# Two of the four weight-side sums of a Strassen product move from VectorE to adding DMAs

## The chip, the cores and the metric

The kernel runs on one core of one Trainium2 chip. The metric is the device time of one execution in microseconds (us): the median of the runs, three of the kernel before. Engines: TensorE (PE; its weight loads are PEld), VectorE (DVE), ScalarE (ACT), GpSimd (POOL) and SyncE (SP), which here issues all DMAs of the kernel before.

## What is computed

One decoder block: RMSNorm of 528 tokens (16 meta tokens and 512), one wide projection `w_in`, two gated branches (differential attention, and a state-space branch with a short convolution and chunked scan, called SSD), one projection each, a gated merge, an output projection and a last RMSNorm. Cut to the matrix products, which are the bulk:

```python
u = rmsnorm(h, norm_g[l])
zp = u @ w_in[l]                       # 2048 x 13344
q, k, v, g_att, z_ssm, xbc, dt, m_att, m_ssm = jnp.split(zp, SPLIT_IDX, axis=-1)
...
y_att = oa @ w_br_attn[l]              # 1024 x 2048
...
y_ssm = yg @ w_br_ssm[l]               # 2048 x 2048
merged = jax.nn.sigmoid(m_att) * y_att + jax.nn.sigmoid(m_ssm) * y_ssm
h = h + merged @ w_out[l]              # 2048 x 2048
return rmsnorm(h[:, N_META:], final_g)
```

## The kernel before, in words

**Jobs.** `plan()` (line 61) lists jobs; each makes 256 output features for all tokens. A job of form "S" is one Strassen-Winograd product (`strassen`, line 211): its weights are cut into A11 A12 / A21 A22, the activations into B11 B12 / B21 B22, and seven products P1 to P7 take the place of eight. The activation sums T1 to T4 are made once per matrix; the weight sums are made per job. Jobs of form "F" (`plain`, line 340) multiply without Strassen: one gate job, all y_att jobs, the first output job. Stages follow each other: attention heads (jobs kv and qg), gates, the convolution (jobs bc and xs), gates and z with the SSD chunks as side work, y_att, y_ssm, output.

**Weights.** Every tile is 128 x 1024 float32, 512 KB, one quadrant A of an S job. `pump` (line 154) loads them in the order of `plan()` from SP into five buffers `w` and never runs more than five ahead of `release` (line 162). A sixth buffer, `S`, holds a running weight sum.

**A unit.** Half a tile (512 columns, four weight blocks of 128) is a unit; a job has 14, two per product, in the order P1 P5 P6 P7 P4 P2 P3 (line 49). A unit has three steps, given out by `dense` (line 416): `sums` (line 225), then at most two units later `prep`, then at most three units later `mm`. `prep` calls `split` (line 166): ACT rounds the weights to a high part `wh` (line 170), DVE subtracts for the low part `wl` (line 171). `mm` (line 322) gives TensorE 12 matmuls, three per weight block (high by high, high by low, low by high), 256 or 264 columns wide. `post` (line 272) takes a product from PSUM and adds it on. `later(fn, n)` (line 384) runs something n units on.

**The weight sums before**, all on DVE, for a usual S job (line 225): at P5, S = A21 + A22 (group S<-w, line 184); at P6, S = S - A11; at P7, A21 = A11 - A21 (group w<-w, line 181); at P3, A12 = A12 - S. Two half-tile instructions each. Two jobs go another way: the first (kv 0, `start`, because activations are not ready) and the last (out 7, `end`); 64 are usual.

**Queues.** DVE, ACT, POOL and SP each work in their own order; a waiting instruction holds those behind it. The order in each queue is set by the build's scheduler, from the order in which the code gives the steps out.

**SSD side work** (line 1032). Per chunk SP loads among others `mm` (line 1023, 512 KB, a row of decay sums given to all 128 partitions) and `ea` (line 1027); ACT turns `mm` into decays (line 1067); `wh` of the next units stands behind it in ACT's order.

Of the kernel before, what the change touches and what calls it, by code (L numbers as in the profile page):

```python
# [10 lines left out]
F32 = mybir.dt.float32  # L11
# [25 lines left out]
C_B, C_C, C_DT, C_MA, C_MS = 8192, 8704, 9216, 9248, 11296  # L37

# [75 lines left out]
def block_kernel(ctx, tc, t_in, out):  # L114
# [35 lines left out]
    WB = 5  # L150
    wt = {}
    wstate = {"next": 0, "done": 0}

    def pump(most=1 << 30):
        while wstate["next"] < min(wstate["done"] + WB, n_tiles, most):
            i = wstate["next"]
            w = wp.tile([P, 1024], F32, tag="w", bufs=WB, name="w")
            sp.dma_start(w, wd[i])
            wt[i] = w
            wstate["next"] += 1  # L160

# [49 lines left out]
    def strassen(ji, width, lo, dst, fin, add=None, end=None, start=False):  # L211
# [7 lines left out]
        order = ORDER_START if start else ORDER_END if end else ORDER  # L219

# [4 lines left out]
        def sums(p, u):  # L225

            us = slice(u * 512, (u + 1) * 512)
            pump()
            if start and p == "P3":
                if u == 0:  # L230
                    st["S"] = wp.tile([P, 1024], F32, tag="S", bufs=1, name="S")
                vsub(block("A21", u), block("A11", u), block("A21", u))
                vsub(st["S"][:, us], block("A22", u), block("A21", u))
                vsub(block("A12", u), block("A12", u), st["S"][:, us])
            elif start:
                if p == "P5":
# [7 lines left out]
            if start:
                pass
            elif p == "P6":
                vsub(st["S"][:, us], st["S"][:, us], block("A11", u))
            elif p == "P7":
                vsub(block("A21", u), block("A11", u), block("A21", u))
            elif p == "P3":  # L250
                vsub(block("A12", u), block("A12", u), st["S"][:, us])

        def prep(p, u):
            pump()
            if p in ("P5", "P6"):
                return split(st["S"][:, u * 512:(u + 1) * 512])
            r = split(block({"P1": "A11", "P7": "A21", "P4": "A22", "P2": "A12", "P3": "A12"}[p], u))
            if u == nu - 1 and not end:
                release(({"P7": 2, "P4": 2} if start else {"P7": 2, "P4": 1, "P3": 1}).get(p, 0))
            return r  # L260
# [11 lines left out]
        def post(p, ps):  # L272
            a = ps[:, :width]
            if p == "P1":
                act.activation(ctile("c1"), a, AF.Copy)
            elif start and p != "P4":
                if p == "P2":
                    vadd(ctile("u3"), a, st["c1"][:, :width])
                elif p == "P3":
                    act.activation(ctile("c5"), a, AF.Copy)  # L280
                elif p == "P6":
                    vadd(ctile("u2"), a, st["c1"][:, :width])
                    d = dst(0, 0)
                    act.activation(d, st["u3"][:, :width], AF.Copy)
                    fin(0, 0, d)
                elif p == "P5":
                    act.activation(ctile("c1"), a, AF.Copy)
                    vadd(ctile("u4"), a, st["u2"][:, :width])
                    quadrant(0, 1, add, st["u4"], st["c5"])
                else:  # L290
                    vadd(ctile("u3"), a, st["u2"][:, :width])
                    quadrant(1, 1, add, st["u3"], st["c1"])
            elif end and p in ("P6", "P7", "P3", "P5"):
                if p == "P6":
                    vadd(ctile("u2"), a, st["c1"][:, :width])
                elif p == "P7":
                    vadd(ctile("u3"), a, st["u2"][:, :width])
                elif p == "P3":
                    vadd(ctile("u4"), a, st["u2"][:, :width])
                    end(0, 1, st["u4"][:, :width])  # L300
                    end(1, 1, st["u3"][:, :width])
                else:
                    for f, b in ((1, "u3"), (0, "u4")):
                        vadd(dst(f, 1), a, st[b][:, :width])
                    for f in (1, 0):
                        fin(f, 1, dst(f, 1))
            elif p == "P5":
                act.activation(ctile("c5"), a, AF.Copy)
            elif p == "P6":
                vadd(ctile("u2"), a, st["c1"][:, :width])  # L310
                add(ctile("u4"), st["u2"][:, :width], st["c5"][:, :width])
            elif p == "P7":
                vadd(ctile("u3"), a, st["u2"][:, :width])
# [5 lines left out]
            else:  # L319
                quadrant(0, 1, vadd, a, st["u4"])  # L320
# [171 lines left out]
    quad_load(("B21", "B22"), HK[1])  # L492

# [130 lines left out]
    def dt_mm(w):  # L624
# [8 lines left out]
        release()  # L633
# [765 lines left out]
```

## Time and profile before

| | |
|---|---|
| median of 3 runs | 1822.39 us (1817.94 to 1826.14) |
| the profiled execution | 1822.93 us, its span 1821.2 us |
| TensorE busy | 1704.3 us, 94% |
| DVE busy | 1647.5 us, 90% |
| ACT busy | 984.7 us, 54% |
| POOL busy | 569.6 us, 31% |
| DMA engines | 41.3% of 16 engines' time, 240.76 MB on SP's queue |
| mean granted clock of TensorE | 0.978 |

Stages in the span, roughly: start 0 to 100 us, attention 100 to 550, gates to 590, convolution to 865, SSD with z and gates to 1370, y_att to 1460, y_ssm to 1630, output to the end. Shares of busy time are means over these stages, so the tables by stretch matter more. Matmuls are pipelined and their ends are modelled: a busy TensorE still tells that work was there, and the count of matmuls per stretch tells how fast it went.

### The profile page before, as it was taken

How to read it: one execution, taken by the hardware profiler on the slowest of the kernel's cores; microseconds unless marked ns; L12 is line 12 of the kernel's file. 1: busy time of each engine (PE TensorE's matmuls, PEld its weight loads, DVE VectorE, ACT ScalarE, POOL GpSimd, SP SyncE). 2: the span in 40 equal slices, each digit the busy share in tenths (PEclk: the TensorE clock that was granted, in tenths of full speed). 3: DMA queues.
4: the chain of work that ended last, by engine and by line, in shares of the span. 5: the costliest groups of instructions: out<-in, count | busy, mean ns of one | idle time of the engine just before them, and what ended most of it. 6: DMA issues, size and time to landing. Idle time of an engine off the chain costs nothing.

```text
span 1821.2 us, 36122 instructions
## 1 busy us (share of the span) xinstructions
PE 1704.3 (94%) x13523; PEld 1628.8 (89%) x13523; DVE 1647.5 (90%) x2914; ACT 984.7 (54%) x2038; POOL 569.6 (31%) x537
## 2 busy tenths in 40 slices
PE   7799999999999999999998999899998999989996
PEld 6799988899999888888987898899997999979995
DVE  8899888889898999999978898999987499998997
ACT  5655554555555544444575556656563254455653
POOL 3333122212212544442133423513432012134444
PEclk9899999999999999999999999999999999989998
DMA  8222222222233333334455555644466644533443
GB/s 308 86 96 83 81 77 86 78 93 75 76 123 99 108 117 116 118 117 137 155 166 153 159 154 161 188 136 137 159 220 226 190 146 153 174 103 105 134 139 104
DMA packets 136767, 243.06 MB, mean 133 GB/s; under 512 B 15088, under 2 KB 78768, under 8 KB 136080
## 3 DMA queue, kind: packets, MB, share of 16 engines
q1 hardware_dynamic: 136592, 240.76, 41.3%
q8 instruction: 106, 1.74, 0.4%
q14 instruction: 69, 0.57, 0.1%
HBM read 206.83 MB, written 33.88 MB: 132 GB/s over the span
## 4 chain that ended last, share of the span: by engine, by line
PE 33%; DVE 8%; DMA 4%; ACT 3%; issue 2%; POOL 1%; SPq 0%; DVEq 0%; ACTq 0%
PE d_ps L331 26%; PE d_ps L370 4%; DVE wl L171 3%; DMA mm<-d_acs 2%; ACT mm L1067 1%; ACT wh L170 1%; PE s_ps L1104 1%; DVE w L181 1%; DMA ea<-d_acs 1%; DVE res L1337 0%; PE s_ps L1080 0%; POOL mq L178 0%; DVE y L455 0%; DVE S L181 0%; DVE x L455 0%
## 5 line engine op out<-in xcount | busy, mean ns | idle before, releaser
L331 PE MATMUL d_ps<-x,wh 128*128 128x256 f32 (+1 forms) x4224 | 780.2, 286 | 12.7 <-ACT wh L170 10.8
L331 PEld LDWEIGHTS d_ps<-x,wh 128*128 128x128 f32 x4224 | 657.3, 191 | 21.2 <-ACT wh L170 15.1
L331 PE MATMUL d_ps<-x,wl 128*128 128x256 f32 (+1 forms) x2112 | 603.1, 288 | 19.0 <-DVE wl L171 18.7
L331 PE MATMUL d_ps<-y,wh 128*128 128x256 f32 (+1 forms) x3168 | 591.3, 286 | 26.3 <-ACT wh L170 26.3
L170 ACT ACTIVATE wh<-w 128x512 fp32r<-128x512 f32 x708 | 427.0, 625 | 344.4 <-PE d_ps L331 165.2
L171 DVE TENSOR_TENSOR wl<-w,wh 128x512 fp32r<-128x512 f32 x708 | 523.3, 757 | 63.2 <-ACT wh L170 61.7
L331 PEld LDWEIGHTS d_ps<-y,wh 128*128 128x128 f32 x3168 | 490.2, 189 | 41.3 <-ACT wh L170 35.0
L331 PE MATMUL d_ps<-y,wl 128*128 128x256 f32 (+1 forms) x1584 | 447.3, 286 | 2.6 <-DVE wl L171 2.5
L331 PEld LDWEIGHTS d_ps<-x,wl 128*128 128x128 f32 x2112 | 400.9, 191 | 27.5 <-DVE wl L171 25.2
L331 PEld LDWEIGHTS d_ps<-y,wl 128*128 128x128 f32 x1584 | 297.3, 189 | 8.4 <-DVE wl L171 5.6
L170 ACT ACTIVATE wh<-S 128x512 fp32r<-128x512 f32 x264 | 163.4, 626 | 128.8 <-PE d_ps L331 62.5
L171 DVE TENSOR_TENSOR wl<-S,wh 128x512 fp32r<-128x512 f32 x264 | 200.1, 775 | 15.6 <-ACT wh L170 14.6
L370 PE MATMUL d_ps<-x,wh 128*128 128x256 f32 x624 | 117.3, 289 | 21.9 <-ACT x L454 8.2
L187 POOL TENSOR_TENSOR gth<-gth,rb 128x256 f32<-128x256 f32 x60 | 67.0, 1121 | 200.0 <-DVE gth L184 148.0
L370 PEld LDWEIGHTS d_ps<-x,wh 128*128 128x128 f32 x624 | 99.5, 196 | 23.1 <-ACT x L454 8.2
L184 DVE TENSOR_TENSOR S<-w 128x512 f32<-128x512 f32 x130 | 104.1, 834 | 2.7 <-DMA w<-in_w_all 2.6
L181 DVE TENSOR_TENSOR S<-S,w 128x512 f32<-128x512 f32 x130 | 106.0, 833 | 0.1
L181 DVE TENSOR_TENSOR w<-w,S 128x512 f32<-128x512 f32 x132 | 102.0, 787 | 0.7
L187 POOL TENSOR_TENSOR raw<-ct,rb 128x8 f32<-128x8 f32 x96 | 85.7, 921 | 44.1 <-DVE ct L184 43.2
L187 POOL TENSOR_TENSOR mq<-mq,cth 128x256 f32<-128x256 f32 x32 | 34.7, 1087 | 198.5 <-DVE mq L184 110.7
L181 DVE TENSOR_TENSOR w<-w 128x512 f32<-128x512 f32 x132 | 96.0, 732 | 0.0
L175 POOL TENSOR_TENSOR u<-u,c 128x264 f32<-128x264 f32 (+1 forms) x27 | 38.7, 1432 | 179.4 <-DVE u L184 122.7
(279 smaller groups left out, 2134.4 us busy)
## 6 DMA issues: line engine op xcount, KB each, us to landing
w<-in_w_all SPq DMA_DIRECT2D x289, 512.0 KB, 3.6
mm<-d_acs SPq DMA_DIRECT2D x16, 512.0 KB, 6.5
d_x<-cv SPq DMA_DIRECT2D x24, 264.0 KB, 2.8
y<-in_x SPq DMA_DIRECT2D x4, 1024.0 KB, 9.2
d_tha<-gth SPq DMA_DIRECT2D x16, 256.0 KB, 2.5
lx<-d_x SPq DMA_DIRECT2D x16, 256.0 KB, 4.8
d_sz<-gth SPq DMA_DIRECT2D x16, 256.0 KB, 3.5
lz<-d_sz SPq DMA_DIRECT2D x16, 256.0 KB, 3.4
```

Of the source, the lines that this page charges most:

```text
L170: act.activation(h[:, :n], src, AF.Copy)
L171: dve.tensor_tensor(l[:, :n], src, h[:, :n].bitcast(F32), ALU.subtract)
L175: pool.tensor_tensor(dst, a, b, ALU.add)
L181: dve.tensor_tensor(dst, a, b, ALU.subtract)
L184: dve.tensor_tensor(dst, a, b, ALU.add)
L187: pool.tensor_tensor(dst, a, b, ALU.mult)
L331: pe.matmul(ps[:, :width], lhsT=a[:, ks], rhs=x[:, kk, lo:lo + width], start=(kk == 0 and i == 0), stop=(kk == kp - 1 and i == 2))
L370: pe.matmul(b[:, :width], lhsT=a[:, cs], rhs=x[:, ki, lo:lo + width], start=(first and k == 0 and i == 0), stop=(last and k == 1 and i == 2))
L1067: act.activation(mm[:, h, :], mm[:, h, :], AF.Relu, scale=-1.0, bias=acs[:, c, g * HPG + h:g * HPG + h + 1])
L1104: pe.matmul(dg[64 * (h % 2):64 * (h % 2) + 64, (h // 2) * P:(h // 2 + 1) * P], lhsT=xdt[:, h * 64:(h + 1) * 64], rhs=mm[:, h, :], start=Tr ...
```

## The change

The signs of the Strassen-Winograd form are turned so that all four weight sums are additions: with A21 and A22 taken as negative, S = A21 + A22, then S + A11, A21 + A11, and A12 + S; the sign comes back in `post`, where some additions become subtractions. Two of the four, A21 + A22 and A21 + A11, are then made by DMAs: SP loads A21 into S (a second time, besides the one into `w`), and four units later a DMA issued by POOL adds A22 from HBM into it; in the same way A11 is added into the `w` tile of A21 four units after its load. The two others stay on DVE, both into S. Tiles are loaded in the order A11, A21, A22, A12 and given back one by one; there are four buffers `w` and two `S` in place of five and one. S is loaded when the P3 of the job two before is split. The first and the last job keep their sums on DVE. The dt tile leaves the stream of weights and is loaded into an S buffer at the start.

```diff
-    WB = 5
-    wt = {}
+    WB = 4
+    wt, ws = {}, {}
...
+    usual = [ji for ji, j in enumerate(jobs) if j[2] == "S" and j[:2] not in (("kv", 0), ("out", 7))]
+    sstate = {"next": 0, "done": -1}
+    A11, A21, A22, A12 = range(4)
...
+    def accumulate(dst, i, key):
+
+        def issue():
+            pool.dma_start(out=dst, in_=wd[i], accum_op=ALU.add)
+            summed_by_dma.add(key)
+        return issue
+
     def pump(most=1 << 30):
-        while wstate["next"] < min(wstate["done"] + WB, n_tiles, most):
-            i = wstate["next"]
+        while wstate["next"] < min(wstate["done"] + WB, len(stream), most):
+            ji, i = stream[wstate["next"]]
             w = wp.tile([P, 1024], F32, tag="w", bufs=WB, name="w")
             sp.dma_start(w, wd[i])
             wt[i] = w
+            t = tiles_of[ji]
+            if ji in usual and i == t[A21]:
+                later(accumulate(w, t[A11], (ji, "P7")), 4)
             wstate["next"] += 1
+
+    def pump_sums():
+        while sstate["next"] < min(sstate["done"] + 2, len(usual)):
+            ji = usual[sstate["next"]]
+            t = tiles_of[ji]
+            ws[ji] = wp.tile([P, 1024], F32, tag="S", bufs=2, name="S")
+            sp.dma_start(ws[ji], wd[t[A21]])
+            later(accumulate(ws[ji], t[A22], (ji, "P5")), 4)
+            sstate["next"] += 1
...
             pump()
+            if mine:
+                if p == "P6":
+                    vadd(ws[ji][:, us], ws[ji][:, us], block("A11", u))
+                    if u == 1:
+                        release()
+                elif p == "P3":
+                    vadd(ws[ji][:, us], ws[ji][:, us], block("A12", u))
+                    if u == 1:
+                        release()
+                return
...
         def prep(p, u):
             pump()
+            if mine:
+                assert p not in ("P5", "P7") or (ji, p) in summed_by_dma, (ji, p)
+                if p in ("P5", "P6", "P3"):
+                    r = split(ws[ji][:, u * 512:(u + 1) * 512])
+                    if p == "P3" and u == 1:
+                        sstate["done"] += 1
+                        pump_sums()
+                    return r
+                r = split(block({"P1": "A11", "P7": "A21", "P4": "A22", "P2": "A12"}[p], u))
+                if u == 1 and p in ("P7", "P4"):
+                    release()
+                return r
...
             elif p == "P6":
-                vadd(ctile("u2"), a, st["c1"][:, :width])
-                add(ctile("u4"), st["u2"][:, :width], st["c5"][:, :width])
+                vsub(ctile("u2"), a, c("c1"))
+                add(ctile("u4"), c("u2"), c("c5"))
             elif p == "P7":
-                vadd(ctile("u3"), a, st["u2"][:, :width])
+                vsub(ctile("u3"), c("u2"), a)
                 quadrant(1, 1, add, st["u3"], st["c5"])
...
             else:
-                quadrant(0, 1, vadd, a, st["u4"])
+                quadrant(0, 1, vsub, a, st["u4"])
...
+    wdt = wp.tile([P, 1024], F32, tag="S", bufs=2, name="wdt")
+    sp.dma_start(wdt, wd[tiles_of[1][0]])
```

The order of instructions, at three places. First DVE in the convolution, most of one job. `S` and `w` are weight tiles, `ct` and `u` sums of products, `cv` a convolved row. Before:

```order
L181 TENSOR_TENSOR w<-w,S 128x512 x2
L184 TENSOR_TENSOR ct<-d_ps,u_9473 128x264
L184 TENSOR_TENSOR S<-w 128x512 x2
L171 TENSOR_TENSOR wl<-w,wh 128x512 x2
L181 TENSOR_TENSOR w<-w 128x512
L171 TENSOR_TENSOR wl<-w,wh 128x512
L181 TENSOR_TENSOR w<-w 128x512
L171 TENSOR_TENSOR wl<-w,wh 128x512
L184 TENSOR_TENSOR ct<-d_ps,c_9345 128x264
L883 SCALAR_TENSOR_TENSOR cv<-raw,c_conv_w,cv 128x528
L171 TENSOR_TENSOR wl<-S,wh 128x512 x2
L184 TENSOR_TENSOR ct<-d_ps,u_9433 128x264
```

and with the change:

```order
L216 TENSOR_TENSOR S<-S,w 128x512
L203 TENSOR_TENSOR wl<-S,wh 128x512
L937 SCALAR_TENSOR_TENSOR cv<-raw,c_conv_w,cv 128x528
L213 TENSOR_TENSOR ct<-d_ps,u_8818 128x264
L216 TENSOR_TENSOR S<-S,w 128x512
L203 TENSOR_TENSOR wl<-S,wh 128x512
L940 SCALAR_TENSOR_TENSOR cv<-cth,cv 128x528
L216 TENSOR_TENSOR S<-S,w 128x512
L203 TENSOR_TENSOR wl<-S,wh 128x512
L203 TENSOR_TENSOR wl<-w,wh 128x512
L937 SCALAR_TENSOR_TENSOR cv<-raw,c_conv_w,cv 128x528
L216 TENSOR_TENSOR S<-S,w 128x512
```

The pairs S<-w and w<-w are gone; four single S<-S,w remain per job, with splits between them.

Second, POOL in the convolution, about one job; `raw` is the unconvolved row that ACT and DVE take up, and what a row waits for stands in brackets (DMAHW: a landing of SP's DMAs, DMASW: of POOL's own). Before:

```order
L175 TENSOR_TENSOR u_8545<-u_8543,c_8501 128x264 [waits DVE_49,Activation_49]
L175 TENSOR_TENSOR ct<-u_8585,c_8501 128x264 [waits DVE_49]
L187 TENSOR_TENSOR raw<-ct,rb 128x8 [waits Pool_49]
L187 TENSOR_TENSOR raw<-ct,rb 128x256
L187 TENSOR_TENSOR raw<-ct,rb 128x8 [waits DVE_49]
L187 TENSOR_TENSOR raw<-ct,rb 128x256
L187 TENSOR_TENSOR raw<-ct,rb 128x8 [waits DVE_49]
L187 TENSOR_TENSOR raw<-ct,rb 128x256
L187 TENSOR_TENSOR raw<-ct,rb 128x8 [waits DVE_49]
L187 TENSOR_TENSOR raw<-ct,rb 128x256
L903 MEMSET raw 128x3 [waits DVE_49,Activation_49] x2
```

and with the change:

```order
L170 DMA w<-in_w_all 128x1024 [waits DMAHW1_49,DMASW7_49]
L957 MEMSET raw 128x3 [waits DVE_49,Pool_49]
L207 TENSOR_TENSOR ct<-u_7679,c_7594 128x264 [waits DVE_49]
L219 TENSOR_TENSOR raw<-ct,rb 128x8 [waits Pool_49]
L219 TENSOR_TENSOR raw<-ct,rb 128x256
L219 TENSOR_TENSOR raw<-ct,rb 128x8 [waits DVE_49]
L219 TENSOR_TENSOR raw<-ct,rb 128x256
L170 DMA S<-in_w_all 128x1024 [waits DMAHW5_49,DMASW6_49,Activation_49]
L219 TENSOR_TENSOR raw<-ct,rb 128x8 [waits DVE_49]
L219 TENSOR_TENSOR raw<-ct,rb 128x256
L957 MEMSET raw 128x3 [waits DVE_49,Activation_49]
```

Two adding DMAs stand among the products, one into `w` and one into `S`; each waits for the landing of its own load.

Third, SP near the first SSD chunks; `mm` and `ea` are the decay loads, `lx`, `lb` a chunk's operands. Before:

```order
L158 DMA w<-in_w_all 128x1024
L1018 DMA lx<-d_x 128x4x128
L593 DMA d_tha<-gth 128x512
L1019 DMA lb<-d_x 128x128
L1020 DMA lb<-d_x 128x128
L158 DMA w<-in_w_all 128x1024
L1023 DMA mm<-d_acs 128x8x128
L158 DMA w<-in_w_all 128x1024
L1027 DMA ea<-d_acs 64x4x128 x2
```

and with the change:

```order
L178 DMA w<-in_w_all 128x1024
L190 DMA S<-in_w_all 128x1024
L1077 DMA mm<-d_acs 128x8x128
L649 DMA d_tha<-gth 128x512
L1072 DMA lx<-d_x 128x4x128
L178 DMA w<-in_w_all 128x1024
L1073 DMA lb<-d_x 128x128
L1074 DMA lb<-d_x 128x128
L649 DMA d_tha<-gth 128x512
L178 DMA w<-in_w_all 128x1024
L1077 DMA mm<-d_acs 128x8x128
L1081 DMA ea<-d_acs 64x4x128 x2
```

A load of S from the weights now stands ahead of a decay load `mm`; the other loads keep their neighbours.

## Rows read from the trace of the kernel before

**Rows 1.** The page: busy us, share of the span, instructions of each engine.

```profile
PE 1704.3 (94%) x13523; PEld 1628.8 (89%) x13523; DVE 1647.5 (90%) x2914; ACT 984.7 (54%) x2038; POOL 569.6 (31%) x537
```

**Rows 2.** Stretches: busy us (x) PE, PEld, DVE, ACT, POOL; clock, DMA share, GB/s.

```profile
100.00:550.00 450.00, 444.26 (x3381) 412.76 (x3380) 400.07 (x897) 252.83 (x574) 100.53 (x116) 1.00 0.27 87
550.00:600.00 50.00, 47.80 (x376) 46.84 (x375) 42.50 (x79) 26.83 (x58) 18.01 (x25) 0.97 0.34 112
600.00:850.00 250.00, 231.26 (x1846) 224.58 (x1847) 249.95 (x389) 124.73 (x221) 115.11 (x125) 1.00 0.35 117
850.00:900.00 50.00, 47.93 (x401) 47.03 (x400) 49.10 (x107) 24.96 (x52) 4.40 (x4) 1.00 0.46 143
900.00:1350.00 450.00, 421.97 (x3374) 395.60 (x3373) 412.21 (x723) 275.54 (x639) 157.45 (x133) 0.97 0.54 163
1500.00:1600.00 100.00, 100.00 (x845) 100.00 (x844) 97.70 (x166) 44.40 (x81) 19.70 (x20) 1.00 0.51 160
1600.00:1650.00 50.00, 42.47 (x310) 40.29 (x309) 49.37 (x67) 24.48 (x38) 19.03 (x11) 0.90 0.38 115
```

**Rows 3.** Groups, whole span, DVE sums: count | busy us, mean ns | idle before.

```profile
L184 DVE TENSOR_TENSOR S<-w 128x512 f32<-128x512 f32 x130 | 104.1, 834 | 2.7 <-DMA w<-in_w_all 2.6
L181 DVE TENSOR_TENSOR w<-w 128x512 f32<-128x512 f32 x132 | 96.0, 732 | 0.0
```

**Rows 4.** Waits, 550 to 900, TensorE: us in total, times, longest us.

```profile
PE d_ps L331 <- ACT wh L170: 13.7, 23, 0.8
PE d_ps L331 <- DVE wl L171: 6.3, 12, 0.7
```

**Rows 5.** DVE groups of conv (600 to 850, x22), then of SSD (900 to 1350, x32).

```profile
L181 DVE TENSOR_TENSOR w<-w,S 128x512 f32<-128x512 f32 x22 | 22.0, 1038 | 0.0
L184 DVE TENSOR_TENSOR S<-w 128x512 f32<-128x512 f32 x22 | 17.9, 851 | 0.0
L181 DVE TENSOR_TENSOR w<-w 128x512 f32<-128x512 f32 x22 | 14.9, 679 | 0.0
...
L181 DVE TENSOR_TENSOR w<-w 128x512 f32<-128x512 f32 x32 | 25.3, 799 | 0.0
L184 DVE TENSOR_TENSOR S<-w 128x512 f32<-128x512 f32 x32 | 24.1, 793 | 0.0
```

**Rows 6.** Waits, 900 to 1350 (SSD), TensorE, then ACT.

```profile
PE d_ps L331 <- ACT wh L170: 15.8, 14, 2.9
PE d_ps L331 <- DVE wl L171: 5.2, 9, 1.4
...
ACT mm L1067 <- DMA mm<-d_acs: 42.6, 15, 4.6
ACT wh L170 <- DVE w L181: 21.9, 14, 5.4
ACT ea L1070 <- DMA ea<-d_acs: 13.3, 10, 3.0
```

**Rows 7.** SP's queue; DMA issues, median us to landing; weight tiles in SSD.

```profile
q1 hardware_dynamic: 136592, 240.76, 41.3%
...
w<-in_w_all SPq DMA_DIRECT2D x289, 512.0 KB, 3.6
mm<-d_acs SPq DMA_DIRECT2D x16, 512.0 KB, 6.5
...
DMA to landing us min/median/max: 3.4/4.1/8.7
```

**Rows 8.** SP's issue of weight tiles (duration ns min/median/max); two POOL groups.

```profile
L158 SPq DMA_DIRECT2D w<-in_w_all x289: 327/328/1497, 1.3 to 1769.9; - x145
...
L175 POOL TENSOR_TENSOR y<-y,lx 128x512 f32<-128x512 f32 x16 | 29.2, 1823 | 47.1 <-DVE y L1107 19.8 <-PE d_ps L331 10.4 <-ACT lx L1072 9.9
L1123 POOL TENSOR_TENSOR sq<-sq,mhalf 128x1 f32<-128x1 f32 x16 | 14.2, 887 | 51.9 <-DVE sq L1122 41.7 <-DMA w<-in_w_all 10.2
```

**Rows 9.** DVE group of the y_ssm stretch, 1500 to 1600.

```profile
L181 DVE TENSOR_TENSOR w<-w,S 128x512 f32<-128x512 f32 x10 | 6.9, 688 | 0.2
```

More of the change, by code (lines that the diff above doesn't have):

```diff
@@ L149, in block_kernel @@
         n_tiles += n
-    WB = 5
-    wt = {}
+    WB = 4
+    wt, ws = {}, {}
     wstate = {"next": 0, "done": 0}
+    usual = [ji for ji, j in enumerate(jobs) if j[2] == "S" and j[:2] not in (("kv", 0), ("out", 7))]
+    sstate = {"next": 0, "done": -1}
+    A11, A21, A22, A12 = range(4)
+    stream = []
+    for ji in range(len(jobs)):
+        if jobs[ji][0] == "dt":
+            continue
+        t = tiles_of[ji]
+        stream += [(ji, i) for i in ([t[A11], t[A21], t[A22], t[A12]] if ji in usual else t)]
+    summed_by_dma = set()
+    def accumulate(dst, i, key):
[3 more added lines that the diff above has]
+        return issue
     def pump(most=1 << 30):
-        while wstate["next"] < min(wstate["done"] + WB, n_tiles, most):
-            i = wstate["next"]
+        while wstate["next"] < min(wstate["done"] + WB, len(stream), most):
+            ji, i = stream[wstate["next"]]
             w = wp.tile([P, 1024], F32, tag="w", bufs=WB, name="w")
@@ L219, in strassen @@
         order = ORDER_START if start else ORDER_END if end else ORDER
+        mine = not (start or end)
         def block(b, u):
@@ new lines, in sums @@
+            if u == 0 and p == ("P3" if start else "P6"):
+                st["S"] = wp.tile([P, 1024], F32, tag="S", bufs=2, name="S")
+            if start and p == "P3":
+                vadd(block("A21", u), block("A11", u), block("A21", u))
+                vadd(st["S"][:, us], block("A22", u), block("A21", u))
+                vadd(block("A12", u), block("A12", u), st["S"][:, us])
+                if u == 1:
+                    pump_sums()
+            elif p == "P5":
+                vsub(st["S"][:, us], st["S"][:, us], block("A11", u))
+            elif end and p == "P6":
@@ L241, in sums @@
                 vadd(st["S"][:, us], block("A21", u), block("A22", u))
-            elif p == "P5":
                 vadd(st["S"][:, us], st["S"][:, us], block("A11", u))
[L244 to L251, printed above, removed]
+            elif end and p == "P7":
+                vadd(block("A21", u), block("A11", u), block("A21", u))
+            elif end and p == "P3":
+                vadd(block("A12", u), block("A12", u), st["S"][:, us])
@@ L253, in prep @@
         def prep(p, u):
             pump()
-            if p in ("P5", "P6"):
-                return split(st["S"][:, u * 512:(u + 1) * 512])
+            if mine:
[4 more added lines that the diff above has]
+                        sstate["done"] += 1
+                        pump_sums()
+                    return r
[3 more added lines that the diff above has]
+                return r
@@ L257, in prep @@
+            if p in ("P5", "P6"):
+                r = split(st["S"][:, u * 512:(u + 1) * 512])
+                if start and p == "P5" and u == 1:
+                    sstate["done"] = 0
+                    pump_sums()
+                return r
             r = split(block({"P1": "A11", "P7": "A21", "P4": "A22", "P2": "A12", "P3": "A12"}[p], u))
-            if u == nu - 1 and not end:
-                release(({"P7": 2, "P4": 2} if start else {"P7": 2, "P4": 1, "P3": 1}).get(p, 0))
+            if start and u == 1:
+                release({"P7": 2, "P4": 2}.get(p, 0))
@@ L532, in meta_squares @@
         dve.memset(ss, 0.0)
-        xw = wp.tile([P, 1024], F32, tag="S", bufs=1, name="S")
+        xw = wp.tile([P, 1024], F32, tag="S", bufs=2, name="S")
         for i in range(2):
@@ L659, in dt_tile @@
     def dt_tile():
-        pump()
-        return wt[tiles_of[job_at["dt", 0]][0]]
+        return wdt
     kv0 = {}
```

40 lines of the change are left out of this document (15 added, 25 removed).

## The prediction

> **What bounds the kernel now.** I read the page's line of busy times first, then a table of stretches, then the waits in the stretches that looked loose. The page [rows 1] shows two engines near the top: TensorE 94% busy and VectorE (DVE) 90%. That average mixes stages with different limits, so the table of stretches decides [rows 2]. In the products of y_ssm (1500 to 1600) TensorE is busy all the time and DVE 97.7%: there TensorE is the bound, and DVE, though nearly full, costs nothing. In the conv stretch (600 to 850) it is the other way round: DVE is busy 249.95 of 250 us and TensorE 231.26. In the attention stretch (100 to 550) TensorE is busy 444.26 of 450. In the SSD stretch (900 to 1350) neither is full, and TensorE loses 28.0 us. At the change of operands (1600 to 1650) DVE is at 49.37 of 50 and TensorE loses 7.5.
>
> The waits say the same: TensorE's idle time before a product ends with one of the two halves of a split, ACT's `wh` or DVE's `wl`, in conv [rows 4] and SSD [rows 6]. In SSD, ACT itself waits for two DMAs, the decay loads `mm` and `ea`: 42.6 + 13.3 us [rows 6].
>
> **The change, part by part.**
>
> *Sums taken off DVE.* 64 products' jobs lose four half-tile sums each, two of the form S<-w and two of the form w<-w: 128 of the 130 and 128 of the 132 in [rows 3], 102.5 + 93.1 = 196 us of DVE. Worth is read per stretch.
>
> *Conv.* DVE loses 17.9 + 14.9 = 32.8 us there [rows 5], so its need falls from 249.95 to 217.2. TensorE's need: a saturated stretch runs 845 matmuls in 100 us [rows 2], 118.3 ns each with 256 columns; for 264 columns that scales to 122 ns (my estimate), times 1846 is 225.2 us. So TensorE becomes the bound, DVE at 217.2/225.2 = 96%, a share at which the y_ssm stretch loses nothing. The stretch holds 22 units S<-w, 11 jobs; conv has 12: at most (250 - 225.2) x 12/11 = 27.1 us. DVE's load here comes in lumps (the taps), so I take -22; bounds -27.1 and 0.
>
> *Attention and the edges.* TensorE idles 5.7 us in attention and 2.2 + 2.1 us in the stretches on both sides of conv [rows 2]; a lighter DVE gives back part: -4 and -2; bounds -10 and 0.
>
> *SSD, DVE's side.* 16 jobs lose 24.1 + 25.3 = 49.4 us of DVE [rows 5] of 412. Of TensorE's idle time, 15.8 + 5.2 = 21.0 us ends with a split [rows 6]; ACT's own waits there are 21.9 us for DVE's sums against 55.9 for DMAs. I take -9; bounds -21 and 0.
>
> *Operands of the output stage.* DVE-bound now; two jobs lose about 3.1 us of DVE each: -3; bounds -6 and 0.
>
> *The DMAs added.* Per job one plain load of 512 KB (A21 into S, on SP) and two adding DMAs of 512 KB (on POOL). How much of the 16 DMA engines does a plain tile take? In attention a share of 27% moves 87 GB/s [rows 2]: 121.5 us for 39 MB, 3.1 us per MB, 1.6 us per tile. No adding DMA is in the trace. From below it is a plain tile, 1.6 us; from above I use the slowest row of that size, the decay load with its small packets, 6.5 us [rows 7] (a landing, so a high bound for engine time). An adding DMA reads two tiles and writes one, where a load reads one and writes one, so I take twice the plain tile, 3.2 us: the plain tile is the nearer row. A job then adds 1.6 + 6.4 = 8.0 us of DMA: in SSD (28.1 us per job) the share goes from 0.54 to 0.82, in the y_ssm stretch (168 x 118.3 ns = 19.9 us per job) from 0.51 to 0.91. Below 1 everywhere, so nothing is bound by it, but loads get slower.
>
> Who feels that? Weight tiles do not: a tile is asked for a whole job ahead. Fourteen units of 12 matmuls are 19.9 us; the adding DMA is issued four units (5.7 us) after its load, whose landing takes 3.6 us (4.1 in SSD) [rows 7], and 14 us are left for it to land; S has longer. If that cover were gone, every late microsecond would stand before a split, twice a job. The decay loads `mm` do feel it: ACT already waits for 15 of 16. At share 0.54 a weight tile lands in 4.1 us, over all in 3.6: 14% for 0.13 of share (0.54 against 41.3% over all) [rows 2, 7]. Another 0.28 of share gives about 30%: 6.5 us grows by 2 us, times 16 is 32 us of ACT. TensorE now loses 21.0 us to splits against ACT's 55.9 us on DMAs, 38%: +12. Bounds 0 and +40 (the load doubled: 16 x 6.5 x 38%).
>
> *POOL's issues.* 128 issues at between SP's 0.33 us and POOL's 1.8 us for a 128x512 sum; nearest is POOL's fixed cost, 0.89 us for a 128x1 power [rows 8]: 114 us, POOL from 31% to 38%. Behind each stand POOL's products for the conv, which ACT's `cv` takes up, and SSD's `y`. An issue first waits for its load, issued 5.7 us earlier: with the slowest landing of SSD, 8.7 us [rows 7], it holds POOL for 3. POOL is idle more than half of each stretch: 0. But POOL and DVE also slow each other: the sum w<-w,S takes 1038 ns in conv, where POOL is busy 46%, and 688 in the y_ssm stretch, where it is busy 20% [rows 2, 5, 9]. Up to 1.8 us per issue, 233 us of DVE, could come back in that way; I take 0, because an issue, unlike POOL's sums, has no tile to read. The Trainium skill ("SBUF — State Buffer", Who interferes with whom) states the rule: a DVE instruction with two SBUF inputs contends with a GpSimd instruction that reads SBUF, not with one that only writes, and it infers that descriptor writing is held up only by DVE's two-port modes, which a tensor_tensor does not have. By that rule the sum stands as it is; by the bound from rows it would lose nearly all its gain (third rival).
>
> *SP and the start.* 64 more issues of 0.33 us on SP, 21 us of 1821; in SSD the decay load now stands behind an S load in SP's order, a third of a microsecond (in the +12). The order of signs and which tile is overwritten cost nothing: the same shapes on the same engines. Four w buffers and two S in place of five and one: a tile is freed by the split or sum that used to free it, or earlier: 0. The dt tile is loaded ahead of the fourth weight tile: 0, bounds -2 and +2.
>
> **Sum**: -22 - 4 - 2 - 9 - 3 + 12 = -28. The profiled execution took 1822.9 us, half a microsecond over the median of the three runs shown, so it may stand for them: **1795 us**.
>
> **Rivals.** (1) *The DMA engines become the bound.* With 9.8 us of DMA free in a y_ssm job, that is from (9.8 - 1.6)/2 = 4.1 us per adding DMA; SSD follows from 5.6. At the upper bound of 6.5 a y_ssm job needs 10.1 + 14.6 = 24.7 in place of 19.9 us (+38 over 8 jobs), an SSD job 15.2 + 14.6 = 29.8 in place of 28.1 (+27 over 16), an output job about 21.3 (+10), conv gains nothing, attention its 4: about **1890**, slower. For it: nothing here shows an adding DMA. Against: it must cost 2.5 plain tiles.
> (2) *The decay loads take the gain.* If `mm` doubles, +40 stands against -40: **1822**, and more if TensorE follows ACT's wait by more than 38%. For it: ACT waits for 15 of 16 of these loads today. Against: the adding DMAs fill a quarter of the time, so most loads meet only one.
> (3) *POOL's issues hold DVE*, as its sums do: 128 x 1.4 us (the middle of 0.89 and 1.8) = 179 of the 196 us return, and only the -4 of the attention remains: **1817**.
> That the sums do not leave DVE is no rival: its order holds them no longer.
>
> **How the numbers follow.** Forecast 0.58, its own range 1766 (nearly all bounds below) to 1812; rival 1 0.14, rival 2 0.20, rival 3 0.08. About 0.5%, 9 us, can be told from no change here: faster means under 1813, slower over 1831. Faster: 0.55 of the forecast, 0.05 of rival 2, 0.03 of rival 3, 0.63; same 0.03 + 0.09 + 0.03 = 0.15; slower 0.14 + 0.06 + 0.02 = 0.22. The range goes on to 1850, through rivals 2 and 3, and leaves out most of rival 1 and little below.
>
> **What would show it.** Right: in conv TensorE busy over 245 of 250 us and DVE no longer full; about 200 us less DVE busy in all; 353 loads from SP; DMA share near 0.8 in SSD and 0.9 in y_ssm; `mm` landing at 8 to 9 us. Wrong: splits or products waiting for DMAs into w or S; y_ssm no longer saturated (rival 1); ACT waiting over 100 us for `mm` (rival 2); DVE's splits longer than today's 757 ns (rival 3).

## The result and the profile after

The changed kernel takes **1835.6 us** (median of 6 runs, 1830.3 to 1837.6) against 1819.0 (6 runs) for the kernel before on the same chip: ratio 1.0079, 95% interval 1.0055 to 1.0102. It is slower by 0.8% where 1.5% faster was forecast. The page of the changed kernel, its busy line, the two queues and the issues of 512 KB (engine, count, KB, median us to landing):

```profile
PE 1699.6 (93%) x13523; PEld 1634.0 (89%) x13523; DVE 1498.7 (82%) x2659; ACT 983.9 (54%) x2038; POOL 611.6 (33%) x664
...
q1 hardware_dynamic: 145808, 274.32, 45.7%
q0 software_dynamic: 18432, 67.12, 22.0%
...
w<-in_w_all SPq DMA_DIRECT2D x288, 512.0 KB, 4.3
S<-in_w_all SPq DMA_DIRECT2D x64, 512.0 KB, 5.7
S<-in_w_all POOLq DMA_DIRECT2D x64, 512.0 KB, 5.8
w<-in_w_all POOLq DMA_DIRECT2D x64, 512.0 KB, 7.5
mm<-d_acs SPq DMA_DIRECT2D x16, 512.0 KB, 6.5
```

DVE is 149 us less busy than in [rows 1], so the sums have left it; the adding DMAs are the new queue q0. The table of stretches (columns as in [rows 2]; the stages now begin up to 20 us earlier or later):

```profile
100.00:550.00 450.00, 450.00 (x3530) 425.65 (x3530) 376.80 (x862) 267.40 (x607) 127.43 (x157) 1.00 0.59 153
...
600.00:850.00 250.00, 227.13 (x1801) 223.03 (x1801) 221.01 (x345) 121.14 (x219) 103.93 (x136) 0.97 0.70 187
900.00:1350.00 450.00, 417.47 (x3298) 394.23 (x3299) 375.45 (x652) 267.02 (x614) 163.16 (x164) 0.95 0.78 213
1500.00:1600.00 100.00, 95.02 (x795) 93.70 (x794) 74.50 (x139) 42.22 (x76) 24.91 (x27) 1.00 0.80 226
```

In conv (600 to 850) DVE is no longer full, 221.01 us, and yet TensorE does less than before, 227.13 against 231.26 us [rows 2]. In y_ssm (1500 to 1600) TensorE has lost the saturation it had, with DVE at 74.5% and the DMA engines at 0.80. So something is late that none of the shares shows. To place it I took the first matmul of each job from the trace; the distances between them, in us, are used for every run below (a few matmuls of output job 0 run ahead of the last of y_ssm and are not taken as its first; the last row is the best kernel of this study). Each row is one profiled execution, for the changed kernel the fastest of its runs (1830.3 us), for e4 the median one and for e5 and e11 the slowest (1795.9 and 1791.9), so differences of a few us between rows mean little:

```
                     start  attention  gates  conv    SSD   y_att  y_ssm  output 0-6
before               102.1    377.2    75.2  276.4  529.1  102.4  172.9  145.5
changed              100.3    361.9    75.5  269.9  547.1  107.3  173.1  151.6
no adding DMA (e4)   102.6    389.2    75.1  276.5  529.9  101.7  172.5  157.3
only S by DMA (e2)   102.4    376.0    76.9  257.3  534.3  103.9  172.3  157.0
only A21 by DMA (e3) 104.5    376.5    75.2  267.4  533.4  101.0  168.9  154.4
both pinned (e5)     110.1    361.2    77.0  259.1  527.6  104.5  163.0  150.3
e11 (best)           101.1    361.7    76.2  259.6  530.6  103.2  162.9  152.0
```

Attention gains 15 us, conv only 6.5, SSD loses 18, the output 6. Within y_ssm the jobs rise from 19.9 to about 21 us, from the third on, and the change of operands gives the loss back.

**What is late: GpSimd's products.** GpSimd's two groups that issue the adding DMAs (line 170), with the idle time before them and its largest releaser:

```profile
L170 POOL DMA_DIRECT2D w<-in_w_all x64 | 56.3, 879 | 468.2 <-DVE wl L203 114.8
...
L170 POOL DMA_DIRECT2D S<-in_w_all x64 | 56.9, 888 | 229.0 <-DMA S<-in_w_all 101.9
```

An issue itself is cheap, 0.88 us. But GpSimd stands idle before it, and for S the releaser is the load that the add goes onto. (For w the profile also names instructions of DVE that had long ended.) The times in the trace settle it for both: 61 of the 64 adds in S and 51 of the 64 in w start 0.5 to 0.7 us after their own load has landed, after idle times that sum to 219 and 458 us. For w these are often longer than the load itself (median 7.9 us against 3.6 from issue to landing): GpSimd stands at the add before the load is even issued, because the ring has no free slot for it yet. GpSimd's order in y_ssm, in time (start, us, instruction, idle before and releaser):

```profile
1517.24 0.88 POOL L170 DMA_DIRECT2D w<-in_w_all  x1 [9.49 <-DMA w<-in_w_all]
1517.85 1.05 POOL L219 TENSOR_TENSOR mq<-mq,cth 128x256 f32<-128x256 f32 x1
1520.37 1.12 POOL L219 TENSOR_TENSOR mq<-mq,cth 128x256 f32<-128x256 f32 x1 [1.47 <-DVE mq L216]
1525.59 0.88 POOL L170 DMA_DIRECT2D S<-in_w_all  x1 [4.10 <-ACT wh L202]
1526.20 1.04 POOL L219 TENSOR_TENSOR mq<-mq,cth 128x256 f32<-128x256 f32 x1
```

The add waits 9.49 us for its load at the head of GpSimd's queue, and the product `mq` behind it starts the moment it is issued. DVE, which needs that product for the next, waits in its turn (1480 to 1600; total, times, longest):

```profile
DVE mq L216 <- POOL mq L219: 30.1, 17, 4.0
```

DVE is idle there with splits of weights queued behind, and TensorE waits for those (5.0 us from 1500 to 1610). It closes to a ring: load, add, product, DVE's split, which frees the slot for the next load. The chain that ended last runs through it, job after job; one round of it (start, us, instruction; pauses under 0.5 us left out):

```profile
1511.68 5.01 DMA w<-in_w_all
1517.24 0.88 POOL w L170
1518.13 0.78 POOL mq L219
1519.28 0.68 DVE wl L203
1519.99 4.76 DMA S<-in_w_all
```

### The profile page after: what moved, and what is told of

It is laid out like the page before. It is cut to its first block, busy times and chain, and to the rows that moved or that the text cites. A ratio compares the mean times of both kernels' runs of the same rounds, so it can differ in the third digit from the quotient of the medians.

```text
span 1828.6 us, 36384 instructions
## 1 busy us (share of the span) xinstructions
PE 1699.6 (93%) x13523; PEld 1634.0 (89%) x13523; DVE 1498.7 (82%) x2659; ACT 983.9 (54%) x2038; POOL 611.6 (33%) x664
## 5 line engine op out<-in xcount | busy, mean ns | idle before, releaser
L385 PE MATMUL d_ps<-x,wl 128*128 128x256 f32 (+1 forms) x2112 | 605.7, 287 | 13.7 <-DVE wl L203 13.3
L203 DVE TENSOR_TENSOR wl<-w,wh 128x512 fp32r<-128x512 f32 x580 | 421.6, 744 | 104.2 <-ACT wh L202 101.2
L202 ACT ACTIVATE wh<-w 128x512 fp32r<-128x512 f32 x580 | 354.5, 626 | 241.0 <-PE d_ps L385 170.3
L385 PEld LDWEIGHTS d_ps<-x,wl 128*128 128x128 f32 x2112 | 403.1, 191 | 23.2 <-DVE wl L203 17.8
L202 ACT ACTIVATE wh<-S 128x512 fp32r<-128x512 f32 x392 | 241.8, 626 | 243.6 <-PE d_ps L385 128.1
L203 DVE TENSOR_TENSOR wl<-S,wh 128x512 fp32r<-128x512 f32 x392 | 311.5, 801 | 56.0 <-ACT wh L202 51.5
L216 DVE TENSOR_TENSOR S<-S,w 128x512 f32<-128x512 f32 x258 | 217.0, 843 | 2.2
L170 POOL DMA_DIRECT2D w<-in_w_all x64 | 56.3, 879 | 468.2 <-DVE wl L203 114.8
L170 POOL DMA_DIRECT2D S<-in_w_all x64 | 56.9, 888 | 229.0 <-DMA S<-in_w_all 101.9
L424 PE MATMUL d_ps<-x,wl 128*128 128x256 f32 x312 | 88.4, 287 | 0.0
L937 DVE SCALAR_TENSOR_TENSOR cv<-raw,c_conv_w,cv 128x528 f32<-128x528 f32 x72 | 54.7, 760 | 24.5 <-ACT cv L943 24.5
L219 POOL TENSOR_TENSOR raw<-ct,rb 128x8 f32<-128x8 f32 x96 | 71.7, 854 | 0.9
```

The source lines that it names most:

```text
L170: pool.dma_start(out=dst, in_=wd[i], accum_op=ALU.add)
L202: act.activation(h[:, :n], src, AF.Copy)
L203: dve.tensor_tensor(l[:, :n], src, h[:, :n].bitcast(F32), ALU.subtract)
L216: dve.tensor_tensor(dst, a, b, ALU.add)
L219: pool.tensor_tensor(dst, a, b, ALU.mult)
L385: pe.matmul(ps[:, :width], lhsT=a[:, ks], rhs=x[:, kk, lo:lo + width], start=(kk == 0 and i == 0), stop=(kk == kp - 1 and i == 2))
```

## The experiments

Two theories stood at the start. **Q**: GpSimd's queue, as just described. **T**: traffic, that is, 128 transfers that fill the DMA engines and slow the other loads. Ratios are to the kernel before, with 95% intervals.

**e1: give the adds out later.**

```diff
-  later(accumulate(w, t[A11], (ji, "P7")), 4)
+  later(accumulate(w, t[A11], (ji, "P7")), 8)
-  later(accumulate(ws[ji], t[A22], (ji, "P5")), 4)
+  later(accumulate(ws[ji], t[A22], (ji, "P5")), 12 if sstate["next"] else 4)
```

> The adding DMAs are the same, but each stands later in GpSimd's order: that of S 12 units after its load instead of 4 (some 18 us instead of 6), that of w 8 instead of 4. Theory Q (GpSimd's queue: an adding DMA stands at its head until its own load has landed, and the products behind it come late): GpSimd's waits for the loads of w and S (157 us in the changed kernel) fall below 30, a y_ssm job goes from 21 back to about 19.9, an out job to 19.7, a conv job from 22.9 to 20 to 21; in all 1795 to 1812 us. Theory T (traffic: 128 transfers of 3.1 us on all 16 DMA engines slow the other loads): the bytes and their share are the same, so the time stays at 1830 to 1840.

1833.0 us, 1.0060 (1.0036 to 1.0084): no gain. But it does not test the queue: the scheduler put the adds back where they were. In the conv stage GpSimd's order is that of the changed kernel, the S add in the middle of a job's eight raw products, and GpSimd still waits 4.6 to 5.8 us at the S adds there. `later` is a wish here, not an order.

**e2, e3, e4: one of the two sums, or neither, by DMA.** In e2 A21 gets A11 on DVE at P7; in e3 S gets A22 on DVE at P5 (its plain load stays); e4 has both. In e2 and e4 the tile A11, which DVE now reads at P7, is also given back there and no longer at P6.

```diff
 # e2 and e4
+  elif p == "P7":
+      vadd(block("A21", u), block("A21", u), block("A11", u))
 # e3 and e4
+  if p == "P5":
+      vadd(ws[ji][:, us], ws[ji][:, us], block("A22", u))
```

> Only the sum in S is added by DMA; A21 gets A11 on DVE as before (128 more DVE sums of about 0.76 us). Theory Q: the waits for S are 102 of GpSimd's 157 us, so most of the loss stays: 1822 to 1834. Theory T: half of the adding transfers gone, so half of their cost and half of DVE's relief: 1822 to 1830. The two differ by the rows, not by the time: with Q the waits of GpSimd for S stay near 100 us and the y_ssm and out jobs stay over 20.5.

> Only A21 gets A11 by DMA; S is still loaded on its own, and A22 is added to it on DVE. Theory Q: the waits for w (55 of 157 us) stay, those for S go: y_ssm and out jobs at about 20 to 20.5, 1812 to 1824. Theory T: like the run with S alone, 1822 to 1830.

> No adding DMA: four ring buffers, the order of tiles and the extra plain load of S stay, both sums are on DVE. Theory Q: the time of the kernel before, 1815 to 1825, conv jobs 22.8, y_ssm and out jobs 19.7 to 20. Theory T: 64 loads more than before remain (a third of the extra traffic), 1822 to 1830. If it is well above 1830, the layout with four ring buffers costs by itself, and neither theory has the cause.

e2 1827.0 us, 1.0021 (1.0010 to 1.0032); e3 1827.2, 1.0028 (1.0009 to 1.0046); e4 **1847.8**, 1.0134 (1.0112 to 1.0155), above both theories. So the layout without any adding DMA (four ring buffers in place of five, 64 more plain loads of S, another order of tiles, A11 held until P7) costs 25 us, in attention and output by 12 each (table above): DVE then waits for tiles of the ring. Which of the four it is was not separated; the changed kernel shares the first three. In e4, DVE's waits (total, times, longest):

```profile
DVE w L213 <- DMA w<-in_w_all: 24.6, 23, 2.7
...
DVE S L213 <- DMA w<-in_w_all: 15.3, 8, 3.2
```

Against that layout the adding DMAs gain 12 us. In attention they gain 27, 13 with either alone. In SSD either alone costs about 4 us, both 17; in conv S alone gains 19 us and both only 7. In these two stages both sums together do worse than one: neither DVE's relief nor a fixed price per transfer would do that.

**e5: pin the adds behind GpSimd's earlier products.**

```diff
-  pool.dma_start(out=dst, in_=wd[i], accum_op=ALU.add)
+  tc.keep_in_program_order(pool.dma_start(out=dst, in_=wd[i], accum_op=ALU.add))
 # and given out 8 (S) and 7 (w) units after their loads instead of 4
```

> The same adding DMAs, but pinned in GpSimd's order behind the products that are given out before them, and given out later (S 8 units after its load, w 7). In the run before, only the units were changed and GpSimd's order stayed almost as it was, so that run tells nothing on the queue; this one moves it: in the conv stage the add in S now stands behind all eight raw products of a job instead of in the middle of them. Theory Q (GpSimd's queue): the stretch of 4.7 us in each conv job in which GpSimd waits at the S add with raw products behind it goes; conv jobs from 22.9 to 20 to 21.4 (stage 270 to 240 to 257), out jobs to 19.7 to 20.5, in all 1795 to 1815 us. Theory T (traffic): nothing changes, 1828 to 1840. If conv and out get faster and the SSD stage stays at 547, both are at work, in different stages: 1805 to 1825.

**1793.4 us**, 0.982 (0.9792 to 0.9847): 42 us under the changed kernel (47 by the ratios, each to the kernel before on its own chip), with the same adds and the same bytes. Only 21 adds in S and 5 in w still start within 0.7 us of their load's landing, after 66 and 68 us of idle time. SSD is back at 527.6, y_ssm at 163.0, conv at 259.1. GpSimd in conv now:

```profile
650.85 0.88 POOL L170 DMA_DIRECT2D w<-in_w_all  x1
651.46 2.23 POOL L219 TENSOR_TENSOR raw<-ct,rb 128x8 f32<-128x8 f32 x4
657.78 0.10 POOL L957 MEMSET raw<- 128x3 f32 x1 [4.09 <-DVE cv L937]
658.08 4.31 POOL L219 TENSOR_TENSOR raw<-ct,rb 128x8 f32<-128x8 f32 x2 [0.20 <-DVE ct L213]
662.33 0.88 POOL L170 DMA_DIRECT2D S<-in_w_all  x1
```

Neither add waits. Theory T alone has fallen: the traffic is all there. The start grew by 10 us, 7 of them in the first job with adds (28.4 us against 21.0). The pin of w's add does that, not the delay: e10 and e13, which pin it too, have 27.9 and 28.3 us there, e13 without any delay, and e9, which does not, has 19.9.

**e6: pinned, but both sums of the SSD stage on DVE.**

```diff
+    s_by_dma = [n not in ("z0 z1 z2 z3 z4 z5 z6 z7 ma4 ma5 ma6 ma7 ms0 ms1 ms2 ms3 ms4 ms5 ms6 ms7".split()) for n in lead]
...
+                if p == "P5" and not s_by_dma[ji]:
+                    vadd(ws[ji][:, us], ws[ji][:, us], block("A22", u))
...
+                elif p == "P7" and not w_by_dma[ji]:
+                    vadd(block("A21", u), block("A21", u), block("A11", u))
```

> As the run with the pinned order, but the 20 jobs of the SSD stage (z, ma4 to ma7, ms) have both sums on DVE, with S loaded plainly. The run with no adding DMA at all had 530 us in this stage against 547 with both. Either theory: the stage returns to 528 to 534, so some 15 us under the run with the pinned order if that one still has 547 there, and no gain if the order mends it. In all 1785 to 1808.

1805.2 us, 0.9887 (0.9856 to 0.9918), the stage 537.9. A miss: without its adds the stage is 10 us longer than in e5. That does not price the adds against DVE's sums, though: e4 has the same sums on DVE in this stage and 529.9 there. TensorE's busy time for the stage's matmuls is 498.6 us in e6 and 490.0 in e4, at mean granted clocks of 0.97 and 0.99. Why was not followed up.

**e7: pinned, S alone by DMA** (e2 with e5's pin).

```diff
+    s_by_dma = [True for n in lead]
+    w_by_dma = [False for n in lead]
...
+            tc.keep_in_program_order(pool.dma_start(out=dst, in_=wd[i], accum_op=ALU.add))
```

> As the run with S alone by DMA (1827 us), with its adds pinned behind the products given out before them. Theory Q: what waits for GpSimd behind the S add goes: 1815 to 1824; the conv stage, where GpSimd waited only 0.6 us per job in that run, stays at 255 to 259. Theory T: 1822 to 1830.

1879.5 us, 1.029 (1.0263 to 1.0316): a miss. Attention rises to 411 and DVE waits 50 us for tiles of the ring; conv (260.1) and SSD (526.2) do not suffer. Why the pin does this only where A21's sum is on DVE was not followed up.

**e8: traffic alone.** e2 and, for each missing add, a plain copy of 512 KB within device memory, read by nothing.

```diff
+  tc.keep_in_program_order(pool.dma_start(out=d_copy[ji % 4], in_=wd[t[A11]]))
```

> The run with S alone by DMA (1827 us, SSD stage 534), and in place of each adding DMA into w GpSimd issues a plain 512 KB copy from device memory to device memory, which waits for no load and which nothing reads: the traffic without the wait at the head of GpSimd's queue and without relief of DVE. Theory T: the SSD stage goes from 534 to 542 to 550 and the total to 1835 to 1845. Theory Q: the stage stays within 3 us of 534, the total at 1825 to 1832 (64 issues of 0.9 us on an engine that is idle more than half of the time).

1858.3 us, 1.0179 (1.0151 to 1.0206), SSD 552.2 against e2's 534.3. DVE's waits for ring tiles in and around SSD rise from 9.0 to 20.1 us, so traffic can cost where the kernel waits for loads, and theory T may be right about a mechanism. It is not shown cleanly: the copies are pinned as well, and e7 shows what a pin can do beside DVE's sums into A21. What decided here it was not, since e5 carries more traffic (q0 22% against 16%) in 65 us less.

**e9, e10: pin and delay one of the two.**

```diff
+  a = pool.dma_start(out=dst, in_=wd[i], accum_op=ALU.add)
+  if key[1] == "P5":        # e9: S;   e10: "P7", w
+      tc.keep_in_program_order(a)
```

> Of the two adding DMAs of a job only that of S is pinned behind GpSimd's earlier products and given out 8 units after its load; that of w stays as in the changed kernel. Theory Q says which wait cost what: GpSimd waited 102 us for the loads of S and 55 for those of w, and in the conv stage only at S. Conv as with both pinned (257 to 262), the SSD stage between 528 and 540, y_ssm between 163 and 171: in all 1798 to 1815 us. Were the gain of pinning an accident of another order, nothing ties it to S: anywhere between 1793 and 1836.

> Only the adding DMA of w is pinned and given out 7 units after its load; that of S stays as in the changed kernel. Theory Q: the conv stage keeps its wait of 4.7 us per job at the S add and stays at 266 to 274, the out stage at 150 or more; in all 1815 to 1832 us, and the gains of the two pins apart sum to about the 42 us of both (1835.6 to 1793.4).

e9 1807.4 us, 0.9916 (0.9890 to 0.9942); e10 1811.8, 0.9936 (0.9916 to 0.9956): the first inside its range, the second 3 us under it, and together 52 us, about what e11 (below) gets from both. But e10 holds a miss: its conv stage fell to 260.7 although GpSimd still waits 36 us for S loads there. The wait alone is not the price; it matters what it moves where. In the changed kernel, DVE in conv shows it:

```profile
674.25 0.76 DVE L937 SCALAR_TENSOR_TENSOR cv<-raw,c_conv_w,cv 128x528 f32<-128x528 f32 x1
674.93 0.42 DVE L213 TENSOR_TENSOR ct<-d_ps,u 128x264 f32<-128x264 f32 x1
675.27 2.57 DVE L216 TENSOR_TENSOR S<-S,w 128x512 f32<-128x512 f32 x1
677.76 0.68 DVE L203 TENSOR_TENSOR wl<-S,wh 128x512 fp32r<-128x512 f32 x1
```

And GpSimd at the same time:

```profile
666.39 3.45 POOL L219 TENSOR_TENSOR raw<-ct,rb 128x8 f32<-128x8 f32 x4
674.58 0.88 POOL L170 DMA_DIRECT2D S<-in_w_all  x1 [4.74 <-ACT wh L202]
675.19 1.20 POOL L219 TENSOR_TENSOR raw<-ct,rb 128x8 f32<-128x8 f32 x2
676.04 0.39 POOL L957 MEMSET raw<- 128x3 f32 x1
676.10 1.18 POOL L219 TENSOR_TENSOR raw<-ct,rb 128x8 f32<-128x8 f32 x2
```

The raw products held up by the add run at 675 us, exactly while DVE makes the sum that the next split waits for, and the sum takes 2.57 us instead of 0.68. It is the products and not the issue: in the whole changed kernel the 172 sums S<-S,w that overlap nothing of GpSimd's take 683 ns on average, the ten that overlap an issue alone 684, the 54 that overlap its two-input instructions alone 1009 and the 19 with both 1922. Over the conv stage, that group in the changed kernel (count | busy, mean ns | idle):

```profile
L216 DVE TENSOR_TENSOR S<-S,w 128x512 f32<-128x512 f32 x47 | 49.1, 1045 | 0.0
```

In e10 it takes 789 ns, in e11 it is:

```profile
L218 DVE TENSOR_TENSOR S<-S,w 128x512 f32<-128x512 f32 x47 | 32.6, 694 | 0.0
```

47 x 0.35 us = 16.5 us of DVE on the way to the splits, for a difference of 10.3 us in the stage. TensorE's waits for DVE's splits in the stage, in the changed kernel and in e11 (total, times, longest):

```profile
PE d_ps L385 <- DVE wl L203: 16.3, 11, 2.4
...
PE d_ps L387 <- DVE wl L205: 8.8, 9, 1.0
```

**e11: both pinned, the first job with adds left as it was.**

```diff
+  if key[0] != usual[0]:
+      tc.keep_in_program_order(a)
```

> As the run with both pinned (1793.4 us), but the first job with adding DMAs (qg0) keeps them as in the changed kernel: there the pinned add came too late for its product (28.4 us for the job against 21.0). Expected: the start back from 110 to 101 to 103 us, the rest as it was: 1784 to 1790. If the first job's loss only moves on to the next, 1791 to 1796.

**1784.5 us**, 0.9786 (0.9767 to 0.9805), 2.1% faster than the kernel before: the version to keep.

**e12, e13: is it the wait, or the other engines' order?** The pin makes the scheduler lay out every engine anew. e12 is e11 with a 128x1 read of each loaded tile on GpSimd where the changed kernel has its adds; e13 is e5 with the delay taken back to 4 units.

```diff
 # e12
+    def peek(t):
+        pool.tensor_tensor(wp.tile([P, 1], F32, tag="pk", bufs=2, name="pk"), t[:, :1], t[:, :1], ALU.add)
...
+                later(lambda t=ws[ji]: peek(t), 4)
...
+                    later(lambda t=w: peek(t), 4)
 # e13, against e5
-                later(accumulate(w, t[A11], (ji, "P7")), 7)
+                later(accumulate(w, t[A11], (ji, "P7")), 4)
-            later(accumulate(ws[ji], t[A22], (ji, "P5")), 8 if sstate["next"] else 4)
+            later(accumulate(ws[ji], t[A22], (ji, "P5")), 4)
```

> The best kernel so far (both adds late and pinned, 1784.5 us) and one thing more: at the places where the adding DMAs of the changed kernel stand, GpSimd reads one column of the freshly loaded tile (128 additions of a 128x1 column, an estimate of 0.3 us each from the 128x8 products). It adds no traffic worth counting and delays no sum; it only makes GpSimd wait at its head for the load, as the changed kernel does. Theory Q: most of the 42 to 51 us come back, 1810 to 1835, with GpSimd's wait at the column for the loads of S and w at 80 us or more. Rival P (the gain came from another order of DVE and ACT that the scheduler happened on, or from the adds' later landing): 1785 to 1797.

> The adds pinned behind GpSimd's earlier products but given out 4 units after their loads, as in the changed kernel: the pin without the delay; GpSimd's order in the conv stage is then that of the changed kernel, with the add in S in the middle of the raw products. Theory Q: the place in the order decides, so 1820 to 1840, GpSimd's waits for S near 100 us. Rival P: 1785 to 1805.

e13: 1828.5 us, 1.0037 (1.0018 to 1.0056): the pin without the delay is worth 7 us, so the place in GpSimd's order decides: 55 of its adds in S and 27 in w still start at their load's landing. e12: 1806.2 us, 0.9905 (0.9879 to 0.9932), below its expected band and above the rival's: 22 of the 51 us come back. Nearly all of that is SSD, 550.6 us against e11's 530.6, and GpSimd's waits at the head are there again (630 us in all, much of it idle time in any case; in SSD, total, times, longest):

```profile
POOL pk L190 <- DMA w<-in_w_all: 102.4, 17, 10.8
POOL pk L190 <- DMA S<-in_w_all: 66.1, 18, 7.6
```

Its conv stage is the fastest of all, 254.3, with the S sums at 740 ns: there the held-up products fall elsewhere. So a wait in conv costs when it moves GpSimd's products onto DVE's sums, and in SSD the waits come with the slow stage again. But 29 of the 51 us do not come back, and e13, whose adds do wait, has 540.9 in SSD: part of e12's 20 us may lie in the order that the scheduler laid out anew, which no run here separates.

How SSD pays is only half clear. The stage of the changed kernel, from its first matmul to the next stage's (columns as in [rows 2]):

```profile
807.60:1354.75 547.15, 503.88 (x3984) 477.32 (x3982) 449.86 (x802) 317.98 (x724) 181.45 (x184) 0.96 0.78 212
```

The same of e11:

```profile
798.61:1329.17 530.56, 495.04 (x3984) 469.10 (x3982) 449.64 (x801) 318.31 (x724) 184.35 (x184) 0.97 0.80 219
```

And of e12:

```profile
791.58:1342.17 550.59, 502.08 (x3983) 476.15 (x3982) 440.54 (x801) 316.57 (x724) 197.98 (x223) 0.95 0.77 210
```

TensorE idles 43.3, 35.5 and 48.5 us; and the same 3984 matmuls take 7 to 9 us longer in the two slow ones, at a mean granted clock of 0.96 and 0.95 against 0.97. The decay loads do not explain it. ACT's waits for them in the changed kernel's stage:

```profile
ACT ea L1124 <- DMA ea<-d_acs: 61.5, 13, 8.7
ACT mm L1121 <- DMA mm<-d_acs: 21.6, 13, 5.5
```

In e11 they are:

```profile
ACT ea L1126 <- DMA ea<-d_acs: 42.5, 13, 5.6
ACT mm L1123 <- DMA mm<-d_acs: 34.9, 15, 7.1
```

83 and 77 us, for stages 17 us apart. What does follow the pin is TensorE's wait for the two halves of a split: 17.8 us in the changed kernel's stage, 7.7 in e5's, 8.8 in e11's. In e12 it is 9.9, so its slow stage is not the changed kernel's over again. Which of GpSimd's products in that stage (`y`, `sq`, `gth`, `state`) starts it was not separated.

## Why the prediction was wrong, point by point

- **The step that failed**: "An issue first waits for its load, issued 5.7 us earlier: with the slowest landing of SSD, 8.7 us, it holds POOL for 3. POOL is idle more than half of each stretch: 0." Two errors. The 5.7 us do not exist: GpSimd reaches the add when its own order allows, and SP issues the load when the slot is free. In the changed kernel most adds start 0.5 to 0.7 us after the landing, with GpSimd idle before them for 4.0 us (S) and 7.9 (w), medians of 61 and 51 adds. And an idle share says nothing of a queue: in y_ssm and conv the products behind the add were due at once. Moving the adds in GpSimd's order (e5) takes 42 us off, e11 51. How much of that is the wait and how much the order around it is open in part: putting the waits back (e12) costs 22.
- "POOL and DVE also slow each other ... I take 0": right for the issues, which hold no DVE instruction (sums beside an issue alone 684 ns, beside nothing 683; splits `wl<-w` 744 against 757 before, `wl<-S` 801 against 775). Rival 3 is out; by its own terms it stood at 1819, not 1817. The Trainium skill ("SBUF — State Buffer", Who interferes with whom) has the contention between DVE's two-input instructions and GpSimd's that read SBUF; the trace agrees, 1009 ns beside GpSimd's two-input instructions against 683. What I missed is that a late issue can move the products that do contend.
- "Four w buffers and two S in place of five and one ... 0": in doubt too. e4 prices that layout, with its extra loads and with A11 held until P7, at 25 us, in attention and output; the adding DMAs of the changed kernel win 12 of it back. It is the likely reason for the 6 us that the output stage lost and no term of mine held; e4 loses 12 there.
- **Conv** -22: it was -6.5. DVE did leave its limit, 221 us against my 217.2, but over the whole stage it fell from 269.3 to 245.0, 24 us of the 36 that twelve jobs' sums took at the rate of [rows 5], since its splits took 10 us more and the sums left to it 4; and TensorE stood at 227, not over 245. With the adds moved, the stage gives -17 (e11), -22 in e12.
- **Attention** -4, at most -10: it was -15. The term was mis-sized; the idle time of TensorE, 5.7 us, does not bound it: the stretch 100 to 550 counts TensorE as busy 444 us before and 450 after, but holds 3381 matmuls before and 3530 after [rows 2]. A busy TensorE was not at its peak there.
- **SSD** -9 + 12: it was +18. `mm` did not slow (6.5 us to landing as before, ACT's wait 42.6 to 21.6); ACT's wait for `ea` rose (13.3 to 61.5). Yet e11 has nearly the same sum of both waits in 17 us less, so the decay loads, and rival 2 with them, were not what decided.
- **The operands** -3: the last y_ssm job, which holds them, went from 33.4 to 28.0, -5.4; but the jobs ahead of it lost as much, which I had at 0.
- **The DMA engines** came out as worked out: 22.0% of 1828.6 us for 128 adds is 3.14 us each, against my 3.2; shares 0.78 and 0.80 against 0.82 and 0.91. Rival 1 is out, though the sign I gave for it, y_ssm no longer saturated, did come: it was the ring through GpSimd. The issue was 0.88 against 0.89.
- DVE's busy time fell by 149 us, not 196. The busy times of groups hold the overlap of neighbouring instructions twice (before, three splits of 0.68 us in a row took 1.90); counted once, the sums that left were 181 us. And DVE's other work grew by 32 us: the two sums left to it by 13, the splits by 9, the rest by 10.

The slower side was among my cases, but under causes (full DMA engines, decay loads) that do not fit the runs. The one that came I had priced at zero; that 1835.6 lies in the wider range, which went to 1850 for those other causes, is luck.

## What to carry to other kernels

A DMA that waits for another DMA should be issued from a queue with nothing behind it, or so late that it never waits; look at what stands behind it, not at how idle the engine is. Where a scheduler orders the queues, giving a step out later may do nothing, as in e1: read the built order, and pin it. And price a change of buffers apart from what it carries: here the layout, as e4 has it, cost 25 us and the adds repaid 12, or, well placed, 63.

## What the runs showed of the hardware

- A DMA that adds 512 KB onto SBUF takes 3.1 us of all 16 engines (22.0% of the span for 128 adds), twice a plain tile (1.6 us, the estimate from [rows 2]), and lands 5.8 (S) or 7.5 us (w) after its issue, medians; the issue holds GpSimd for 0.88 us and DVE not at all (sums of 684 ns beside it, 683 beside nothing).
- In SSD, 8 to 13 us more idle time of TensorE came with 7 to 9 us more for the same matmuls, at a mean granted clock of 0.95 to 0.96 against 0.97: the stage grew by 17 to 20 us, about twice the gaps. That the gaps brought the lower clock is not shown.
- A DVE sum of 128x512 rose from 0.68 to 2.57 us beside four small GpSimd products.
